# Interleaved activation tiles and weight units stored back to front in a two-layer encoder trunk

## The chip, the cores and the metric

The kernel runs on one core of a Trainium2 chip. A core has a matrix engine (TensorE, PE in the profile, with its weight loads shown as PEld), VectorE (DVE), ScalarE (ACT), GpSimd (POOL) and SyncE (SP), which issues most of the DMAs. The metric is the device time of one execution in microseconds, the median over several runs.

## The reference

The input is one sequence of 256 rows with 2048 channels, in float32. Two layers follow each other:

```python
u = rms_norm(h, g);  q, k, v, f = split(u @ a_w_in)            # layer A
o = forgetting_attention(q, k, v, cumsum(log_sigmoid(f + b)))  # 16 heads of 128
h = h + o @ a_w_out
h = h + square(relu(rms_norm(h, g) @ w1)) @ w2                 # 2048 -> 8192 -> 2048
k_sh, v_sh = split(rms_norm(h, g) @ kv_w)                      # shared by layer B
q = rms_norm(rms_norm(h, g) @ b_w_q)                           # layer B
h = h + chunked_relbias_attention(q, k_sh, v_sh, b_rel) @ b_w_out
h = h + square(relu(rms_norm(h, g) @ w1)) @ w2
```

Nearly all the work is in the projections with 2048 x 2048 blocks of weights. All of it is float32, and the result must be close to a float32 reference, which decides how the products are formed.

## The kernel before

**Splitting.** A float32 number is split in two parts: hi, the number rounded to the matrix engine's faster 32-bit format (float32r), and lo, the rest. A product of activations x and weights w is then three passes: x_hi with w_hi, x_lo with w_hi, x_hi with w_lo. The function `passes` (L485 to L495) issues them: L491, L493 and L495 in this order. The stationary operand, put into the array by a weight load before each matmul, is a 128 x 128 slice of the activations; the moving operand is a 128 x 512 slice of the weights; the result is a 128 x 512 accumulator.

**Activation tiles.** Activations lie transposed in tiles `[P, 2, GH, T]`: 128 partitions, two parts (hi, then lo), four row groups of 128 channels, 256 sequence positions. Four tiles hold the 16 row groups of one activation, and 60 tiles are made in all. They are filled at five places: `split_x` (L279, input, at the very start, one row group at a time just before its first use), `split_turned` (L312, the activations after each normalisation), `values` (L662, attention output), `take` (L870, the hidden activations of an MLP) and `gates` (L739, not an activation but the small gate weights). ScalarE writes hi, VectorE computes lo as the difference, reading hi again. A weight load reads 128 neighbouring positions of one part and one row group. In `gates` the tiles are the moving operand (L758).

**Weight units.** Weights arrive by DMA in units of 128 x 1024 (`raw`, `UN` = 1024), two slices of 512. `issue` (L213) takes the next unit, lets ScalarE copy it rounded into `hi` (L227) and VectorE subtract into `lo` (L228), in three rotating buffers each, and puts the pair into the queue `ready`. `top_up` and `fetch` keep two to three split units ahead of the matmuls. `products` (L499) applies a plain unit to two blocks of 128 rows: two slices, two blocks, three passes, twelve matmuls.

**Formed units.** In the MLPs and the query projection, blocks of weights are combined in pairs by a seven-product scheme (class `Pair`, `form_products`, L518). For a part of the rows the weights are first added to each other (L848, or a DMA that adds), and such a sum is a formed unit (`Form`), split by the same two lines of `issue` under the names `w`, `wT` and `query`. Its stationary operands are the activation tiles in three of the seven products and sums of activations (`S`, `Sh`) in the other four. The pairs are 1536 wide (14 in all, formed over the first six row groups, the rest plain), 2048 wide (16, over the first eight) or 1024 wide (4, over the first four).

**Order.** The order of all units is written out by `plan_mlp`. Work beside the matmuls (norms, softmax, transposes) is put in small steps into the list `fill`, and one step is run after each unit. At the end `keep_order` fixes the written order of VectorE, ScalarE, TensorE and SyncE; the waits between engines come from the framework, which sees which instruction writes and reads which tile.

Of the kernel before, what the change touches and what calls it, by code (L numbers as in the profile page):

```python
# [10 lines left out]
F32R = mybir.dt.float32r  # L11
# [4 lines left out]
P = 128  # L16
T = 256
# [4 lines left out]
GH = 4  # L22
# [5 lines left out]
UN = 1024  # L28
# [22 lines left out]
def trunk(ctx: ExitStack, tc: tile.TileContext, xT, xr, gs, hg, bf, wgate, w_in, w_oa, w1a, w1fa, w1sa, w2fa, w2sa,  # L51
          w_kv, w_qb, w_ob, w1b, w1fb, w1sb, w2fb, w2sb, rel, out):
    nc = tc.nc
    V, S, G, TE, SY = nc.vector, nc.scalar, nc.gpsimd, nc.tensor, nc.sync

    def pool(name, bufs, **kw):
        return ctx.enter_context(tc.tile_pool(name=name, bufs=bufs, **kw))
# [3 lines left out]
    acts = pool("acts", 8)  # L61
# [33 lines left out]
    first = sm.tile([P, GH], F32, name="first", bufs=1)  # L95
# [100 lines left out]
    tail_b = Tail(w_ob, n_out - 5)  # L196
    plan_b = plan_mlp(w1b, w1fb, w1sb, w2fb, w2sb, tail_b)
    ready = deque()

    raws = deque()  # L200

# [11 lines left out]
    def issue(parts=1):  # L213
        form = None
        if not raws:
            load(parts)
        raw, cuts = raws.popleft()
        if not cuts:
            form, half = raw, raw.half
            raw, cuts = form.pair.t[form.name], [slice(0, form.pair.cols - UN if half else UN)]  # L220
            if half:
                raw = raw[:, UN:]
        n = cuts[-1].stop
        hi = wsp.tile([P, n], F32R, name="hi" if n == UN else "hih", bufs=3 if n == UN else 1)
        lo = wsp.tile([P, n], F32R, name="lo" if n == UN else "loh", bufs=3 if n == UN else 1)
        for c in cuts:
            S.activation(hi[:, c], raw[:, c], AF.Copy)  # L227
            V.tensor_tensor(lo[:, c], raw[:, c], hi[:, c].bitcast(F32), op=ALU.subtract)  # L228
        ready.append((hi, lo, n < UN))
        if form and form.pair.deep and form.name == "T3":  # L230
            make(form.pair, "T2", int(half))
        elif form and half == form.pair.wide:
            if form.name == "T3":
                make(form.pair, "T2")
            elif form.name == "T2" and form.pair.adds:
                put(form.pair, "T4")
# [33 lines left out]
        return [ps_acc.tile([P, 512], F32, name="acc", tag=f"acc{which}{b}", bufs=1) for b in range(NB)]  # L270

    part = [None]

    def quarter(m):
        if m % GH == 0:
            part[0] = acts.tile([P, 2, GH, T], F32R, name="act")
        return part[0][:, :, m % GH, :]

    def split_x(src, m, which):  # L279
# [29 lines left out]
    def room(tag, name, dtype=F32):  # L309
        return qkv.tile([P, DEEP], dtype, name=name, tag=tag, bufs=1)  # L310

    def split_turned(t, n, which, into, fs=None):  # L312
        x = acts.tile([P, 2, GH, T], F32R, name="act")
        y = room("bias", "y").rearrange("p (a t) -> p a t", a=GH)[:, :, :T]
        for j in range(GH):
            m = which * KT + GH * n + j
            S.activation(y[:, j].rearrange("p (b i c) -> p b i c", b=NB, i=4), t[:, j], AF.Copy, scale=gsb[:, m : m + 1])
            if j == 1:
                yield
        S.activation(x[:, 0], y, AF.Copy)  # L320
        V.tensor_tensor(x[:, 1], y, x[:, 0].bitcast(F32), op=ALU.subtract)  # L321
        into.extend(x[:, :, j, :] for j in range(GH))
        yield
        if fs is not None:
            w = (GH - 2 * n) * T
            fs.extend(qkv.tile([P, w], F32R, name="S", tag="sS"[n], bufs=2) for _ in range(2))
            yield from sums([[y[:, j : GH - 2 * n : 2, b * P : (b + 1) * P] for j in range(2)] for b in range(NB)], fs[2 * n :], 2 - n)
# [157 lines left out]
    def passes(items, hi, lo, cols=slice(0, 512), **kw):  # L485

        def cut(w, j):
            return w[:, j * 512 + cols.start : j * 512 + cols.stop]

        for ps, (xh, _), j, first, _ in items:  # L490
            TE.matmul(ps[:, cols], xh, cut(hi, j), start=first, stop=False, **kw)  # L491
        for ps, (_, xl), j, _, _ in items:
            TE.matmul(ps[:, cols], xl, cut(hi, j), start=False, stop=False, **kw)  # L493
        for ps, (xh, _), j, _, last in items:
            TE.matmul(ps[:, cols], xh, cut(lo, j), start=False, stop=last, **kw)  # L495
# [206 lines left out]
    x = []  # L702
# [35 lines left out]

    def gates(x, st):  # L739
        r3 = wgr.rearrange("p (k c) -> p k c", k=KT)  # L740
        w = acts.tile([P, 2, GH, T], F32R, name="act")
        w3 = w.rearrange("p i a t -> p (i a t)").rearrange("p (k c) -> p k c", k=KT)
        box = []

        def clear():
            G.memset(w.bitcast(F32), 0.0)
            G.memset(early[:H, 3 * T : 4 * T], 1.0)

        def parts():
            h3, l3 = w3[:, :, :H], w3[:, :, 32 : 32 + H]  # L750
            S.activation(h3, r3, AF.Copy)
            V.tensor_tensor(l3, r3, h3.bitcast(F32), op=ALU.subtract)

        def products(ks):
            if not box:
                box.append(ps_s.tile([P, 512], F32, name="s"))
            for k in ks:
                TE.matmul(box[0], w3[:, k], x[k], start=k == 0, stop=k == KT - 1)  # L758

        c = early[:H, 2 * T : 3 * T]  # L760

        def logs():
            z = wk.tile([H, T], F32, name="gz", tag="wk")
            u = wk.tile([H, T], F32, name="gu", tag="wk")
            S.activation(z, box[0][:H, T:], AF.Copy)
            V.tensor_tensor(u, box[0][:H, :T], z, op=ALU.add)
            S.activation(z, box[0][32 : 32 + H, :T], AF.Copy)
            V.tensor_tensor(u, u, z, op=ALU.add)
            V.tensor_tensor(u, u, st.R[:H, :], op=ALU.mult)
            V.tensor_scalar(u, u, bfb, None, op0=ALU.add)  # L770
            V.scalar_tensor_tensor(z, u, -1.0, u, op0=ALU.mult, op1=ALU.max)
            yield
            S.activation(z, z, AF.Exp, scale=-1.0)
            S.activation(z, z, AF.Ln, bias=1.0)
            yield
            V.scalar_tensor_tensor(z, u, 0.0, z, op0=ALU.min, op1=ALU.subtract)
            V.tensor_tensor_scan(c, early[:H, 3 * T : 4 * T], z, 0.0, op0=ALU.mult, op1=ALU.add)
            yield
            nct = wk.tile([H, REL], F32, name="nct", tag="wk")
            V.tensor_scalar(nct[:, 0:P], c[:, 0:P], -1.0, None, op0=ALU.mult)  # L780
            V.tensor_scalar(nct[:, P:], c, -1.0, None, op0=ALU.mult)
            ct["cd"] = dram.tile([H, REL], F32, name="cd")
            G.dma_start(ct["cd"], nct)
            yield

        def turn_c():
            pc = ps_o.tile([P, 512], F32, name="pt", tag="po")
            ct["cq"] = const.tile([P, NB, H], F32, name="cq")
            for b in range(NB):
                TE.transpose(pc[:, b * H : (b + 1) * H], c[:, b * P : (b + 1) * P], ident[:H, :H])  # L790
            V.tensor_copy(ct["cq"].rearrange("p b h -> p (b h)"), pc[:, : NB * H])

        step, spread = steps(logs), steps(st.spread)
        return [[clear], [], [parts], [lambda: products(range(8))], [lambda: products(range(8, KT))], [spread], [spread],
                [step], [step], [step], [step], [turn_c]]
# [69 lines left out]
    def mlp(plan, x, Sx, st, last, more=None):  # L865
# [3 lines left out]

        def take(t, c, n):  # L870
            S.activation(t, t, AF.Relu)
            y = acts.tile([P, 2, GH, T], F32R, name="act")
            hi, lo = (y[:, i].rearrange("p k (b i c) -> p (k b) i c", b=NB, i=4) for i in range(2))
            t3 = t.rearrange("p (i kb c) -> p kb i c", i=4, c=32)
            yield
            S.activation(hi, t3, AF.Square)
            yield
            S.activation(t, t, AF.Square)
            yield

            def low():
                V.tensor_tensor(lo, t3, hi.bitcast(F32), op=ALU.subtract)

            hids[c].extend(y[:, :, j, :] for j in range(GH))
            low()
            yield
            if n == 0:
                r = prob.tile([P, 4 * UN], F32R, name="Sh", tag="p", bufs=1)
                Sh[c].extend(r[:, i : i + n] for i, n in ((0, UN), (UN, UN), (2 * UN, UN), (3 * UN, UN)))
                yield from sums([[t3[:, 2 * j + b :: 4] for j in range(2)] for b in range(NB)], Sh[c])  # L890
            elif n == 1:
                yield from sums([[t3[:, 2 * j + b :: 4] for j in range(2)] for b in range(NB)], Sh[c][2:])
# [34 lines left out]
        for i, (p, q, u) in enumerate(plan):  # L927
            hi, lo = ready.popleft()[:2] if q > 1 and ready and not p.deep else fetch()
# [185 lines left out]
```

## Time and profile before

| what | value |
|---|---|
| median of 2 runs | 2098.87 us (2098.66 to 2099.08) |
| profiled execution, first to last instruction | 2090.4 us |
| median above the profiled execution's span | 8.5 us |
| TensorE matmuls | 9182, busy 2076.3 us |
| weight loads | 9182, busy 1709.6 us |
| VectorE busy | 1679.5 us |
| ScalarE busy | 1288.4 us |
| mean DMA rate | 261 GB/s |

The page of the profile gives for each engine its busy time and its share of the span. Matmuls are pipelined, so the lengths of neighbours overlap; the distance between two starts is the better measure of TensorE's pace. A group of instructions is told with its line, engine, operation, what it writes and reads by the program's names, its shape, its count, its busy time, the mean length of one in ns, and after the bar the time for which the engine sat idle just before, with what ended it.

### The profile page before, as it was taken

The numbers are of one execution on the slowest core, as the hardware profiler recorded it, in microseconds if no ns is written. First come the engines' busy times: TensorE is split into PE (matmuls) and PEld (weight loads), VectorE is DVE, ScalarE is ACT, GpSimd is POOL, SyncE is SP. The second block draws the span as 40 slices with busy tenths as digits, with TensorE's granted clock in tenths as the row PEclk, the third lists the DMA queues.
The fourth block names the chain that finished last, engine by engine and source line by source line (L and its number), as shares of the span: only waits on it lengthen the run. The fifth ranks groups of instructions, "written<-read, shape, count | busy, mean of one in ns | idle before, by whom it ended". The sixth has DMA issues, their size and how long they took to land.

```text
span 2090.4 us, 26489 instructions
## 1 busy us (share of the span) xinstructions
PE 2076.3 (99%) x9182; PEld 1709.6 (82%) x9182; DVE 1679.5 (80%) x1972; ACT 1288.4 (62%) x1613; POOL 150.1 (7%) x195
## 2 busy tenths in 40 slices
PE   9999999999999999999999999999999999999999
PEld 7888888878887887887878888888788788878877
DVE  5767666889789889889988577778988897898886
ACT  6544454767567667667776445556765675676674
POOL 1111000001001001001011001000010010010010
PEclk9999999999999999999999999999999999999999
DMA  7777778789689789788878777787987986897885
GB/s 285 248 253 240 232 255 264 250 268 296 232 292 283 241 270 298 231 273 287 280 252 269 233 232 234 247 264 266 294 280 233 284 284 232 291 286 237 274 279 182
DMA packets 176151, 545.14 MB, mean 261 GB/s; under 512 B 37760, under 2 KB 70416, under 8 KB 163728
## 3 DMA queue, kind: packets, MB, share of 16 engines
q1 hardware_dynamic: 163088, 477.31, 64.4%
q0 software_dynamic: 12640, 65.57, 16.2%
q8 instruction: 72, 1.18, 0.2%
q14 instruction: 63, 0.52, 0.1%
q10 hardware_dynamic: 288, 0.57, 0.1%
HBM read 503.49 MB, written 35.68 MB: 258 GB/s over the span
## 4 chain that ended last, share of the span: by engine, by line
PE 86%; DVE 5%; DMA 5%; ACT 2%; issue 2%; SPq 1%; ACTq 0%; DVEq 0%
PE acc L491 22%; PE acc L493 22%; PE acc L495 22%; PE s L495 6%; PE s L491 5%; PE s L493 5%; DVE lo L228 3%; DMA turn<-z 2%; DMA raw<-in_w1sa 1%; ACT hi L227 1%; PE s L635 1%; PE po L665 1%; DVE z L341 1%; DMA raw<-in_w1sb 1%; SPq L357 0%
## 5 line engine op out<-in xcount | busy, mean ns | idle before, releaser
L228 DVE TENSOR_TENSOR lo<-raw,hi 128x1024 fp32r<-128x1024 f32 (+1 forms) x542 | 655.2, 1214 | 189.3 <-ACT hi L227 176.1
L227 ACT ACTIVATE hi<-raw 128x1024 fp32r<-128x1024 f32 (+1 forms) x542 | 569.3, 1053 | 311.3 <-PE acc L493 232.4
L491 PE MATMUL acc<-hi,act 128*128 128x512 f32 x2092 | 580.4, 394 | 1.3 <-ACT hi L227 1.3
L495 PE MATMUL acc<-lo,act 128*128 128x512 f32 x2092 | 571.6, 390 | 0.0
L493 PE MATMUL acc<-hi,act 128*128 128x512 f32 x2092 | 571.0, 389 | 0.1
L493 PEld LDWEIGHTS acc<-hi,act 128*128 128x128 f32 x2092 | 392.7, 188 | 83.0 <-DVE act L321 0.7
L495 PEld LDWEIGHTS acc<-lo,act 128*128 128x128 f32 x2092 | 391.3, 188 | 84.6 <-DVE lo L228 3.4
L491 PEld LDWEIGHTS acc<-hi,act 128*128 128x128 f32 x2092 | 390.5, 188 | 82.0 <-ACT hi L227 3.2
L227 ACT ACTIVATE hi<-w 128x1024 fp32r<-128x1024 f32 x202 | 212.7, 1057 | 93.4 <-PE acc L493 42.9
L228 DVE TENSOR_TENSOR lo<-w,hi 128x1024 fp32r<-128x1024 f32 x202 | 245.5, 1219 | 22.4 <-ACT hi L227 19.1
L228 DVE TENSOR_TENSOR lo<-wT,hi 128x1024 fp32r<-128x1024 f32 x142 | 172.2, 1221 | 60.8 <-ACT hi L227 59.1
L227 ACT ACTIVATE hi<-wT 128x1024 fp32r<-128x1024 f32 x142 | 148.1, 1055 | 74.4 <-PE acc L493 32.2
L495 PE MATMUL s<-lo,act 128*128 128x512 f32 x370 | 102.1, 392 | 6.0 <-DVE lo L228 6.0
L491 PE MATMUL s<-hi,act 128*128 128x512 f32 x370 | 101.1, 390 | 0.0
L493 PE MATMUL s<-hi,act 128*128 128x512 f32 x370 | 100.9, 389 | 0.0
L495 PEld LDWEIGHTS s<-lo,act 128*128 128x128 f32 x370 | 68.7, 188 | 23.8 <-DVE lo L228 10.1
L493 PEld LDWEIGHTS s<-hi,act 128*128 128x128 f32 x370 | 69.5, 188 | 14.4
L491 PEld LDWEIGHTS s<-hi,act 128*128 128x128 f32 x370 | 69.3, 188 | 14.5 <-ACT hi L227 0.3
L848 DVE TENSOR_TENSOR wT<-wT,w 128x1024 f32<-128x1024 f32 (+1 forms) x48 | 66.3, 1381 | 1.6
L668 ACT ACTIVATE act<-po 128x256 fp32r<-128x256 f32 x32 | 12.3, 385 | 88.0 <-PE po L666 88.0
L848 DVE TENSOR_TENSOR wT<-w,w 128x1024 f32<-128x1024 f32 (+1 forms) x48 | 65.5, 1364 | 0.3 <-DMA w<-in_w2fa 0.3
L577 POOL TENSOR_TENSOR ss<-ss,mhalf 128x4 f32<-128x4 f32 x32 | 43.5, 1367 | 271.8 <-DVE ss L576 271.8
(209 smaller groups left out, 1968.8 us busy)
## 6 DMA issues: line engine op xcount, KB each, us to landing
raw<-in_w_in SPq DMA_DIRECT2D x95, 512.0 KB, 4.6
raw<-in_w1sa SPq DMA_DIRECT2D x70, 512.0 KB, 6.4
raw<-in_w1sb SPq DMA_DIRECT2D x70, 512.0 KB, 6.1
w<-in_w2fa SPq DMA_DIRECT2D x32, 1024.0 KB, 7.7
raw<-in_w2sa SPq DMA_DIRECT2D x64, 512.0 KB, 8.0
raw<-in_w_kv SPq DMA_DIRECT2D x64, 512.0 KB, 4.7
w<-in_w2fb SPq DMA_DIRECT2D x32, 1024.0 KB, 7.5
raw<-in_w2sb SPq DMA_DIRECT2D x64, 512.0 KB, 7.3
```

The costliest lines, as they stand in the source:

```text
L227: S.activation(hi[:, c], raw[:, c], AF.Copy)
L228: V.tensor_tensor(lo[:, c], raw[:, c], hi[:, c].bitcast(F32), op=ALU.subtract)
L341: V.transpose(z.rearrange("p (j n b c) -> p b n j c", j=4, n=n, b=nb)[:, b], src.rearrange("p (n j c) -> p n j c", n=n, j=4))
L491: TE.matmul(ps[:, cols], xh, cut(hi, j), start=first, stop=False, **kw)
L493: TE.matmul(ps[:, cols], xl, cut(hi, j), start=False, stop=False, **kw)
L495: TE.matmul(ps[:, cols], xh, cut(lo, j), start=False, stop=last, **kw)
L577: G.tensor_tensor(rn, vv, mhalf, op=ALU.pow)
L635: TE.matmul(s[:, P : 3 * P], q[:, a, P:T], k[:, a], start=True, stop=True)
L665: TE.matmul(po[:, :T], v[:, 0, a * P : (a + 1) * P], pT[:, :2], start=True, stop=False)
L668: S.activation(o[i][:, 0], po[:, :T], AF.Copy)
L848: V.tensor_tensor(d, a, b, op=ALU.add)
```

## The change

Two layouts are altered. First, a helper `new_act` makes the activation tiles, and every second one is laid out as `[P, GH, T, 2]`: the hi and the lo part of one element lie next to each other. The code sees it through a view with the old order of axes, so one part is read and written with a step of two elements. The tile in `gates` keeps its layout and stays in the same rotation. Second, plain weight units of the whole width are counted, and where the count leaves 0 or 1 after division by four, `hi` and `lo` are replaced by views that run backwards. ScalarE and VectorE then store the unit back to front, and the matmuls read it back to front, so that the elements come in the same order as before. These matmuls are issued by a copy of the three loops in `passes`, on lines of their own. The number of instructions, the order of the work, the buffers and the DMAs in the code are the same.

```diff
@@ -196,6 +196,7 @@
     tail_b = Tail(w_ob, n_out - 5)
     plan_b = plan_mlp(w1b, w1fb, w1sb, w2fb, w2sb, tail_b)
     ready = deque()
+    count, back = [0], {}
 
     raws = deque()
 
@@ -223,6 +224,11 @@
         n = cuts[-1].stop
         hi = wsp.tile([P, n], F32R, name="hi" if n == UN else "hih", bufs=3 if n == UN else 1)
         lo = wsp.tile([P, n], F32R, name="lo" if n == UN else "loh", bufs=3 if n == UN else 1)
+        if n == UN and not form:
+            count[0] += 1
+            if count[0] % 4 < 2:
+                hi, lo = hi[:, ::-1], lo[:, ::-1]
+                back[id(hi)] = hi
         for c in cuts:
             S.activation(hi[:, c], raw[:, c], AF.Copy)
             V.tensor_tensor(lo[:, c], raw[:, c], hi[:, c].bitcast(F32), op=ALU.subtract)
@@ -270,10 +276,18 @@
         return [ps_acc.tile([P, 512], F32, name="acc", tag=f"acc{which}{b}", bufs=1) for b in range(NB)]
 
     part = [None]
+    kinds = [0]
+
+    def new_act():
+        i = kinds[0] % 2
+        kinds[0] += 1
+        if i:
+            return acts.tile([P, GH, T, 2], F32R, name="alt", tag="act").rearrange("p a t i -> p i a t")
+        return acts.tile([P, 2, GH, T], F32R, name="act", tag="act")
 
     def quarter(m):
         if m % GH == 0:
-            part[0] = acts.tile([P, 2, GH, T], F32R, name="act")
+            part[0] = new_act()
         return part[0][:, :, m % GH, :]
 
     def split_x(src, m, which):
@@ -310,7 +324,7 @@
         return qkv.tile([P, DEEP], dtype, name=name, tag=tag, bufs=1)
 
     def split_turned(t, n, which, into, fs=None):
-        x = acts.tile([P, 2, GH, T], F32R, name="act")
+        x = new_act()
         y = room("bias", "y").rearrange("p (a t) -> p a t", a=GH)[:, :, :T]
         for j in range(GH):
             m = which * KT + GH * n + j
@@ -487,6 +501,14 @@
         def cut(w, j):
             return w[:, j * 512 + cols.start : j * 512 + cols.stop]
 
+        if id(hi) in back:
+            for ps, (xh, _), j, first, _ in items:
+                TE.matmul(ps[:, cols], xh, cut(hi, j), start=first, stop=False, **kw)
+            for ps, (_, xl), j, _, _ in items:
+                TE.matmul(ps[:, cols], xl, cut(hi, j), start=False, stop=False, **kw)
+            for ps, (xh, _), j, _, last in items:
+                TE.matmul(ps[:, cols], xh, cut(lo, j), start=False, stop=last, **kw)
+            return
         for ps, (xh, _), j, first, _ in items:
             TE.matmul(ps[:, cols], xh, cut(hi, j), start=first, stop=False, **kw)
         for ps, (_, xl), j, _, _ in items:
@@ -738,7 +760,7 @@
 
     def gates(x, st):
         r3 = wgr.rearrange("p (k c) -> p k c", k=KT)
-        w = acts.tile([P, 2, GH, T], F32R, name="act")
+        w = acts.tile([P, 2, GH, T], F32R, name="act", tag="act")
         w3 = w.rearrange("p i a t -> p (i a t)").rearrange("p (k c) -> p k c", k=KT)
         box = []
 
@@ -869,7 +891,7 @@
 
         def take(t, c, n):
             S.activation(t, t, AF.Relu)
-            y = acts.tile([P, 2, GH, T], F32R, name="act")
+            y = new_act()
             hi, lo = (y[:, i].rearrange("p k (b i c) -> p (k b) i c", b=NB, i=4) for i in range(2))
             t3 = t.rearrange("p (i kb c) -> p kb i c", i=4, c=32)
             yield
```

## The prediction

> **What bounds the kernel now.** First the page's busy times and the granted clock, then the chain that ended last, then what TensorE waited for.
>
> ```profile
> span 2090.4 us, 26489 instructions
> PE 2076.3 (99%) x9182; PEld 1709.6 (82%) x9182; DVE 1679.5 (80%) x1972; ACT 1288.4 (62%) x1613; POOL 150.1 (7%) x195
> ...
> PEclk9999999999999999999999999999999999999999
> ...
> PE 86%; DVE 5%; DMA 5%; ACT 2%; issue 2%; SPq 1%; ACTq 0%; DVEq 0%
> ```
>
> ```profile
> PE s L495 <- DVE lo L228: 7.0, 10, 0.9
> PE acc L491 <- ACT hi L227: 1.3, 1, 1.3
> PE pt L92 <- DVE mhalf L94: 1.1, 1, 1.1
> ```
>
> TensorE is busy 99% of the span at the full clock, and its listed waits are 7.0 + 1.3 + 1.1 = 9.4 us. So the time is a count of matmuls times the distance from one start to the next. That distance is read in the timeline of a steady stretch (columns: start, length of the group, engine, line, operation, count). Matmul lengths overlap, so I take starts.
>
> ```profile
> 302.23 1.07 PE L495 MATMUL acc<-lo,act 128*128 128x512 f32 x4
> 303.13 1.07 PE L491 MATMUL acc<-hi,act 128*128 128x512 f32 x4
> 304.04 1.07 PE L493 MATMUL acc<-hi,act 128*128 128x512 f32 x4
> 304.95 1.07 PE L495 MATMUL acc<-lo,act 128*128 128x512 f32 x4
> ```
>
> From 302.23 to 304.95 there are twelve starts: 2.72 / 12 = 0.2267 us, 227 ns per matmul. Times 9182 that is 2081 us, the whole span. The share that grows with the number of columns comes from two shapes of one line:
>
> ```profile
> L493 PE MATMUL acc<-hi,act 128*128 128x512 f32 x2088 | 570.1, 390 | 0.1
> L493 PE MATMUL acc<-hi,act 128*128 128x256 f32 x4 | 0.8, 283 | 0.0
> ```
>
> 256 more columns take 107 ns, so 512 take 214 ns, and about 13 ns of the 227 do not depend on the columns. Weight loads run beside this stream:
>
> ```profile
> 300.18 0.87 PEld L491 LDWEIGHTS acc<-hi,act 128*128 128x128 f32 x4
> 301.10 0.87 PEld L493 LDWEIGHTS acc<-hi,act 128*128 128x128 f32 x4
> ```
>
> ```profile
> 299.74 0.38 PE L634 MATMUL s<-k,q 128*128 128x128 f32 x2
> 299.85 0.30 PEld L635 LDWEIGHTS s<-k,q 128*128 128x128 f32 x2
> ```
>
> ```profile
> L634 PE MATMUL s<-k,q 128*128 128x128 f32 x64 | 12.2, 272 | 0.0
> ...
> L635 PEld LDWEIGHTS s<-k,q 128*128 128x128 f32 x64 | 9.7, 192 | 0.0
> ```
>
> Among long matmuls four loads of 188 ns fill 0.87 us, one per 227 ns, at the matmuls' pace. Among the short ones of the attention, two loads fill 0.30 us, so their starts lie 0.30 - 0.19 = 0.11 us apart, and so do the matmuls' (0.38 - 0.27). A load thus needs at most 110 ns of its own; beside a 512-column matmul it has 227 - 110 = 117 ns to spare.
>
> **The change part by part.** It adds no instruction, DMA or queue entry and moves none; SP's and POOL's queues carry the same items in the same order. It alters the addresses of operands.
>
> How many are touched follows from the loops and these rows:
>
> ```profile
> L228 DVE TENSOR_TENSOR lo<-raw,hi 128x1024 fp32r<-128x1024 f32 x538 | 652.6, 1218 | 188.3 <-ACT hi L227 175.1 <-PE acc L493 9.3 <-PE s L493 0.7
> ...
> L228 DVE TENSOR_TENSOR lo<-raw,hi 128x512 fp32r<-128x512 f32 x4 | 2.6, 686 | 1.0 <-ACT hi L227 1.0
> ```
>
> 538 whole units and two written in halves are 540 plain units; two of every four are 270. Each feeds twelve matmuls (three passes, two slices, two row blocks): **3240 matmuls** read their moving operand backwards. Activation tiles come in fours, and the second and fourth are interleaved. Plain units meet these in 112 of 224 units outside the planned pairs, 84 of 140 in the 1536-wide pairs (row groups 6 to 15 of 16), 64 of 128 in the 2048-wide ones (8 to 15) and 32 of 48 in the narrow ones (4 to 15): 292 units, 3504 weight loads. The second halves of the formed units add 14 x 9 + 16 x 18 = 414. So **3918 weight loads** step by 8 bytes.
>
> *Step of 8 bytes in a weight load.* No row here has such a load. Below: nothing, as now. It may double to 220 ns and still fit into 227. At four times, 440 ns, the pace would be its own: 213 ns x 3918 = +835 us. A gain is limited to the 13 fixed ns, 3918 x 13 = -51 us. I take 0: nearest is the load of at most 110 ns, which would have to more than double before anything shows. If that cover were gone, each further 10 ns would cost 39 us.
>
> [...]
>
> *Moving operand backwards.* No matmul of the trace reads so; two other engines do. VectorE copies the identity reversed (L477), beside a plain copy source of the same size (L467), and ScalarE reads the query room forwards for one normalisation and backwards for the other, eight times each (L317; shortest, median, longest):
>
> ```profile
> L477 DVE COPY flipper<-ident x1: 221/221/221, 1074.8 to 1074.8; 128x128 f32<-128x128 f32 x1
> ```
>
> ```profile
> L467 DVE COPY rb<-rx x2: 218/220/221, 48.0 to 48.1; 128x128 f32<-128x128 f32 x2
> ```
>
> ```profile
> L317 ACT ACTIVATE y<-query,gsb x16: 491/494/497, 1066.4 to 1124.4; 128x256 f32<-128x256 f32 x16
> ```
>
> 221 beside 220 ns, and 491 to 497 over both directions: a backward read is free there. Those engines take one element per ns or so, TensorE one per 107 / 256 = 0.42 ns, so the rows do not prove it for TensorE. Bounds: 0, and half the rate, 214 ns x 3240 = +693 us; a gain is again limited to the fixed part, 3240 x 13 = -42 us. I take 0, by these rows. Eight of the sixteen gate matmuls (L758) get an interleaved moving operand; at half rate that is 8 x 214 ns = 1.7 us.
>
> *Writes.* 270 times ScalarE writes hi and VectorE writes lo backwards, and 30 of the 60 activation tiles are written, and hi read again, with the step of 8 bytes.
>
> ```profile
> L227 ACT ACTIVATE hi<-raw 128x1024 fp32r<-128x1024 f32 x538 | 567.0, 1056 | 310.4 <-PE acc L493 232.4 <-PE s L493 31.6 <-DMA raw<-in_w_in 13.5
> ```
>
> ```profile
> L882 DVE TENSOR_TENSOR act<-q,act 128x1024 fp32r<-128x1024 f32 x32 | 39.1, 1223 | 12.6 <-ACT q L878 11.8 <-DMA w<-in_w2fb 0.8
> ```
>
> L882 reads its source in blocks of 32 and takes 1223 ns, as long as L228 with straight operands (1218): the time goes by element, not by address. I take 0 here too. At half the rate the 270 lo would add 270 x 1.2 = 324 us to VectorE. Outside the MLP that is covered; inside it is not:
>
> ```profile
> core 0: us, PE busy (x) PEld busy (x) DVE busy (x) ACT busy (x) POOL busy (x), PEclk, DMA share, GB/s
> ...
> 440.00:640.00 200.00, 197.60 (x863) 160.77 (x862) 172.08 (x180) 130.11 (x147) 11.71 (x17) 1.00 0.84 271
> 640.00:840.00 200.00, 199.32 (x875) 163.30 (x875) 172.53 (x174) 131.81 (x145) 16.66 (x26) 1.00 0.86 275
> ```
>
> VectorE has some 27 us idle in each 200. An MLP has 12 + 70 + 64 = 146 plain units in about 650 us, 73 of them reversed, 22 per 200 us: 22 x 1.2 = 27 us more would use up all of it.
>
> *Waits.* Interleaved halves of one tile cover the same address range. If the ordering treats that range as one, TensorE's first pass, which needs only hi, also waits for VectorE's lo. Later stages have their tiles long before use; only at the start does a tile come just in time, and only two of its four tiles are interleaved: four steps by the length of L284, 0.48 us, are 1.9 us at most:
>
> ```profile
> L284 DVE SCALAR_TENSOR_TENSOR act<-xin,gsb,act 128x256 fp32r<-128x256 f32 x16 | 7.0, 480 | 4.5 <-ACT act L283 4.5
> ```
>
> Queued behind such a wait on TensorE are only the later matmuls, which are the path itself. I take 1 us of it.
>
> **The sum.** 2090.4 + 0 + 0 + 0 + 1 = 2091.4 us of span. The median of 2098.87 is 8.5 us over the profiled span, so **2100 us**: no change that could be measured. About 2% (42 us) is what a measurement of this kernel can tell from none.
>
> **The rivals.**
>
> *Loads disturb the stream (ends slower).* The 13 fixed ns may be the weight load's reads taking turns with the moving operand's. If twice the span of addresses takes twice the turns, every strided load adds 13 ns: 3918 x 13 = 51 us, **2151 us**, +2.4%. It decides as soon as the extra passes 42 us / 3918 = 11 ns. For it: the fixed part is the same in every clean group. Against it: no row has a different load beside a long matmul. [...]
>
> *The backward stream is slower.* From one more fixed part per matmul (3240 x 13 = +42 us, 2142) to half rate (+693 us, **2793**), with anything between: a quarter of the rate lost, 71 ns each, gives 2330. For it: TensorE takes elements more than twice as fast as the engines whose backward reads are shown. Against it: those rows show no cost at all.
>
> *Backward writes slow VectorE.* At half rate the MLP has no VectorE time left; if half of 2 x 73 x 1.22 = 178 us comes through, 89 us, **2190 us**. Against it: L882 beside L228.
>
> *Strided loads take over twice their time.* At four times, +835 us, about **2935 us**. Against it: the spare 117 ns.
>
> *Faster.* Only the fixed part and the waits can go: 51 us or 42 us, at best about **2050 us**. Nothing in the profile speaks for it.
>
> *The change does not do what it says*, if the reversed view were undone in storing: then nothing changes, and the time is the forecast's.
>
> **How the numbers follow.** No change 0.38 (own range 2090 to 2112); loads disturb the stream 0.18; slower backward stream 0.22, of which 0.12 below 2400; slower writes 0.10; loads over twice 0.06; faster 0.06, half of that within 2%. The single likeliest case is no change, so 2100 is the time, though the slower cases together hold more. A range from 2085 to 2400 holds 0.38 + 0.18 + 0.12 + 0.10 + 0.03 = 0.81. Over 2% slower: 0.18 + 0.22 + 0.06 and 0.08 of the writes are 0.54; over 2% faster 0.03; within 2% the rest, 0.43.
>
> **What would show it.** The reversed matmuls have lines of their own (L506, L508, L510, 1080 each), the others L513, L515, L517. Right: starts 227 ns apart on both sets of lines, L227 and its VectorE partner still near 1056 and 1218 ns, waits of TensorE near 9 us. Loads that disturb: some 240 ns between starts on half of both sets. A slower stream: only L506 to L510 stretch. Slower writes: TensorE's wait for lo grows tenfold and VectorE passes 90% in the MLP. The forecast is wrong if TensorE's reads cost by address rather than by element; that is the step with the least evidence.

## The result and the profile after

The changed kernel takes 2127.65 us (2127.34 to 2127.96), before 2098.87 us: a ratio of 1.0144, 95% interval 1.0115 to 1.0174. That is slower, clear of noise, and less than 2%. The profiled execution lasted 2125.6 us from first to last instruction and 2127.34 us in all.

First the page of the changed kernel, with the busy times and the granted clock, then what its TensorE waited for (us in total, times, longest).

```profile
span 2125.6 us, 26489 instructions
PE 2114.3 (99%) x9182; PEld 1737.8 (82%) x9182; DVE 1680.2 (79%) x1972; ACT 1290.9 (61%) x1613; POOL 151.5 (7%) x195
...
PEclk9999999999999999999999999999999999999999
...
L234 DVE TENSOR_TENSOR lo<-raw,hi 128x1024 fp32r<-128x1024 f32 (+1 forms) x542 | 655.4, 1214 | 202.2 <-ACT hi L233 196.8
L233 ACT ACTIVATE hi<-raw 128x1024 fp32r<-128x1024 f32 (+1 forms) x542 | 569.0, 1052 | 325.8 <-PE acc L515 134.0
```

```profile
PE s L517 <- DVE lo L234: 4.4, 8, 0.9
PE acc L506 <- ACT hi L233: 1.2, 1, 1.2
PE pt L92 <- DVE mhalf L94: 1.1, 1, 1.1
```

The instructions are the same in number, the granted clock is the same (1.000 in both), TensorE is still busy 99% of the span, and it waits less (6.7 us) than before (9.4 us). VectorE and ScalarE split a plain unit in 1214 and 1052 ns, before in 1214 and 1053, although half of these are now written backwards. So TensorE waits for nothing longer: the matmuls themselves follow each other more slowly. The timeline of the changed kernel shows it. L506 to L510 read backwards, L513 to L517 forwards; `act` is an old activation tile, `alt` an interleaved one.

```profile
262.43 1.10 PE L508 MATMUL acc<-hi,act 128*128 128x512 f32 x4
263.36 1.10 PE L510 MATMUL acc<-lo,act 128*128 128x512 f32 x4
264.29 1.09 PE L513 MATMUL acc<-hi,act 128*128 128x512 f32 x4
265.22 1.07 PE L515 MATMUL acc<-hi,act 128*128 128x512 f32 x4
266.12 1.07 PE L517 MATMUL acc<-lo,act 128*128 128x512 f32 x4
267.03 0.59 PE L687 MATMUL po<-pbuf,v 128*128 128x256 f32 x2
...
268.62 1.09 PE L515 MATMUL acc<-hi,alt 128*128 128x512 f32 x4
269.55 1.09 PE L517 MATMUL acc<-lo,alt 128*128 128x512 f32 x4
270.49 1.10 PE L506 MATMUL acc<-hi,alt 128*128 128x512 f32 x4
271.42 1.10 PE L508 MATMUL acc<-hi,alt 128*128 128x512 f32 x4
272.36 0.86 PE L510 MATMUL acc<-lo,alt 128*128 128x512 f32 x3
```

Forwards from old tiles, 265.22 to 267.03, eight matmuls take 1.81 us, 226 ns each. Backwards from old tiles, 262.43 to 264.29, eight take 1.86 us, 233 ns each. With interleaved tiles it is 233 to 234 ns in both directions (268.62 to 272.36, sixteen in 3.74 us). Over the trace from 13 us on, for matmuls of 512 columns that are followed by one of the same kind, distance from start to start:

```
changed kernel            pairs   median ns   mean ns (without gaps over 260 ns)
forwards,  old tile        1887   227         227.9
forwards,  interleaved     1957   233         233.3
backwards, old tile        1368   233         233.4
backwards, interleaved     1606   233         233.5
forwards,  sums (S, Sh)    1232   227         228.5
```

In the trace of before, old tiles and sums both have 227 ns. An interleaved tile costs 6.7 ns, a backward unit costs 6.7 ns, and a matmul that has both pays once. By the counts of the trace 1500 matmuls read backwards with an old tile, beside the 3918 strided loads: 5418 x 6.67 = 36 us. The two profiled spans differ by 2125.6 - 2090.4 = 35.2 us. The medians differ by less, 28.8 us; the profiled execution before was among its faster ones, as more runs of that kernel show below.

Two small things stand beside it, both in the changed kernel: ScalarE's writes with the step of 8 bytes, and the gate matmuls, whose moving operand is an activation tile (for these the three numbers are shortest, median and longest in ns).

```profile
L898 ACT ACTIVATE alt<-q 128x1024 fp32r<-128x1024 f32 x16 | 18.6, 1162 | 0.0
L898 ACT ACTIVATE act<-q 128x1024 fp32r<-128x1024 f32 x16 | 16.8, 1047 | 0.1
```

```profile
L904 DVE TENSOR_TENSOR alt<-q,alt 128x1024 fp32r<-128x1024 f32 x16 | 19.6, 1227 | 14.1 <-ACT q L900 14.1
L904 DVE TENSOR_TENSOR act<-q,act 128x1024 fp32r<-128x1024 f32 x16 | 19.5, 1219 | 0.0
```

```profile
L780 PE MATMUL s<-act x8: 387/392/399, 40.8 to 47.1; 128*128 128x512 f32 x8
...
L780 PE MATMUL s<-alt,act x8: 615/629/630, 41.7 to 48.6; 128*128 128x512 f32 x8
```

An interleaved tile takes ScalarE 115 ns longer to write and VectorE 8 ns; the list of TensorE's waits above shows none for it. In the timeline the gate matmuls whose moving operand has a step of 8 bytes start 448 ns apart (four in 1.79 us, from 41.75 us on), before 227: some 220 ns longer, on eight matmuls, 1.8 us in all.

### The profile page after: what moved, and what is told of

Read it like the earlier page. It is cut to its first block, busy times and chain, and to the rows that moved or that the text cites. A ratio compares the mean times of both kernels' runs of the same rounds, so it can differ in the third digit from the quotient of the medians.

```text
span 2125.6 us, 26489 instructions
## 1 busy us (share of the span) xinstructions
PE 2114.3 (99%) x9182; PEld 1737.8 (82%) x9182; DVE 1680.2 (79%) x1972; ACT 1290.9 (61%) x1613; POOL 151.5 (7%) x195
## 4 chain that ended last, share of the span: by engine, by line
PE 86%; DMA 5%; DVE 4%; ACT 2%; issue 1%; SPq 0%; ACTq 0%; DVEq 0%
PE acc L515 14%; PE acc L513 14%; PE acc L517 14%; PE acc L506 9%; PE acc L510 9%; PE acc L508 9%; PE s L517 4%; PE s L513 4%; PE s L515 4%; DVE lo L234 2%; PE s L506 2%; PE s L510 2%; PE s L508 2%; DMA turn<-z 1%; DMA raw<-in_w1sa 1%
## 5 line engine op out<-in xcount | busy, mean ns | idle before, releaser
L234 DVE TENSOR_TENSOR lo<-raw,hi 128x1024 fp32r<-128x1024 f32 (+1 forms) x542 | 655.4, 1214 | 202.2 <-ACT hi L233 196.8
L233 ACT ACTIVATE hi<-raw 128x1024 fp32r<-128x1024 f32 (+1 forms) x542 | 569.0, 1052 | 325.8 <-PE acc L515 134.0
L513 PE MATMUL acc<-hi,act 128*128 128x512 f32 x598 | 170.6, 395 | 0.0
L517 PE MATMUL acc<-lo,act 128*128 128x512 f32 x598 | 167.4, 390 | 0.0
L515 PE MATMUL acc<-hi,act 128*128 128x512 f32 x598 | 167.3, 390 | 0.1
L513 PE MATMUL acc<-hi,alt 128*128 128x512 f32 x576 | 162.9, 398 | 0.0
L517 PE MATMUL acc<-lo,alt 128*128 128x512 f32 x576 | 161.2, 395 | 0.0
L515 PE MATMUL acc<-hi,alt 128*128 128x512 f32 x576 | 161.0, 394 | 0.0
L506 PE MATMUL acc<-hi,alt 128*128 128x512 f32 (+1 forms) x490 | 136.6, 401 | 0.0
L510 PE MATMUL acc<-lo,alt 128*128 128x512 f32 (+1 forms) x490 | 135.0, 397 | 0.0
L508 PE MATMUL acc<-hi,alt 128*128 128x512 f32 (+1 forms) x490 | 134.4, 396 | 0.0
L513 PEld LDWEIGHTS acc<-hi,act 128*128 128x128 f32 x598 | 111.6, 188 | 25.3 <-ACT hi L233 0.5
L515 PEld LDWEIGHTS acc<-hi,act 128*128 128x128 f32 x598 | 112.2, 188 | 24.6 <-DVE act L335 0.5
L517 PEld LDWEIGHTS acc<-lo,act 128*128 128x128 f32 x598 | 111.9, 188 | 24.0 <-DVE lo L234 0.5
L517 PEld LDWEIGHTS acc<-lo,alt 128*128 128x128 f32 x576 | 111.0, 193 | 23.6 <-DVE lo L234 0.7
L515 PEld LDWEIGHTS acc<-hi,alt 128*128 128x128 f32 x576 | 111.2, 193 | 23.2 <-DVE alt L335 0.2
L513 PEld LDWEIGHTS acc<-hi,alt 128*128 128x128 f32 x576 | 111.1, 194 | 21.6 <-ACT hi L233 0.3
L506 PE MATMUL acc<-hi,act 128*128 128x512 f32 x428 | 120.0, 403 | 1.2 <-ACT hi L233 1.2
```

## The experiments

**The two halves, and the whole again.** Theory A: each matmul with a strided load or a backward operand pays 6.67 ns, once. Rival B: the two costs are separate and add up. Rival C: the backward units carry all of it. Interleaving alone:

```diff
-            if count[0] % 4 < 2:
+            if False:
```

> Interleaved tiles alone; all weight units forwards. Theory A (in the changed kernel's trace a matmul starts 233.3 ns after the last, not 226.7, when its weight load steps by 8 bytes or its moving operand runs backwards, and 233.3 also when both hold): 3918 loads x 6.67 ns = +26 us over before. Theory B (the two costs are separate and add up to the whole of +29 us, in proportion to 3918 and 3240): +16 us. Theory C (the backward units carry it, by their matmuls or their writers): 0.

Backward units alone:

```diff
-        if i:
+        if False:
             return acts.tile([P, GH, T, 2], F32R, name="alt", tag="act").rearrange("p a t i -> p i a t")
```

> Backward units alone; all activation tiles in the old layout. Theory A: 3240 matmuls x 6.67 ns = +22 us. Theory B: +13 us. Theory C: +29 us. Under A the two runs together come to 48 us, about 12 us (1746 matmuls that are both) more than the whole change; under B they come to the whole change.

The changed kernel without an edit, on the same chip:

> The changed kernel again, beside the two halves on one chip. Theory A: 3918 + 1500 = 5418 matmuls x 6.67 ns = +36 us, less what stalls elsewhere give back. Theories B and C: +29 us.

Against 2095.63 us before (eleven runs from 2090.77 to 2100.73), interleaving alone took 2115.93 us, ratio 1.0096 (1.0079 to 1.0113), +20 us; backward units alone 2114.69 us, ratio 1.0087 (1.0071 to 1.0102), +19 us; both 2127.13 us, ratio 1.0150 (1.0130 to 1.0170), +31.5 us. Each is 3 to 6 us under theory A. Rival C falls: interleaving alone costs. The halves come to 39 us, 8 us more than the whole. That is the side of theory A (12 us more) and not of B (nothing more), but the intervals, some 4 us to either side, do not settle it. In the trace of interleaving alone the interleaved loads have 233.3 ns from start to start and the rest 227; in that of backward units alone it is the backward matmuls that have 233.5.

**All units backwards, without and with interleaved tiles.** This sets the two readings far apart: if the costs add, interleaving on top of 540 backward units costs another 26 us; if a matmul pays once, 3 us.

```diff
-            if count[0] % 4 < 2:
+            if True:
```

The first of the two runs has the old layout of the tiles besides.

> All 540 plain weight units backwards, all activation tiles in the old layout: 6480 matmuls. Theory A (6.67 ns per touched matmul): 6480 x 6.67 = +43 us over before. A cost that came from alternating between the two directions would not grow: +20 us as with half of the units.

> All plain units backwards and every second tile interleaved. Theory A (a matmul that has both pays once): only the 414 strided loads of the formed units come on top of all units backwards, 414 x 6.67 = 3 us: +46 us. Rival (the two costs add): 3918 x 6.67 = 26 us on top: +69 us.

Against 2094.89 us before: all backwards 2131.3 us, ratio 1.0169 (1.0155 to 1.0183), +36 us; all backwards and interleaved 2135.06 us, ratio 1.0190 (1.0176 to 1.0204), +40 us. Interleaving adds 4 us, not 26: a matmul pays once. The doubled dose of backward units costs 36 us where half cost 19, so it is no matter of changing direction. Both stand 6 to 7 us under the 43 and 46 of theory A. In the traces, starts more than 260 ns apart exceed 230 ns by 24 us in all before, and by 17 and 18 us in these two. So some 5 to 7 us of stalls went, about what is missing. Slower matmuls leaving the other engines more time is a likely reason; it was not tried by itself.

**The matmul by itself.** Only matmuls on resident data, 24 of a kind on a line of its own, one weight load before each:

```python
for i in range(R): TE.matmul(ps, st(1, i), mv(1, 512), start=True, stop=True)    # L46
for i in range(R): TE.matmul(ps, st(2, i), mv(1, 512), start=True, stop=True)    # L47
...                                                                              # L48 to L50: stationary steps 4, 8, 3
for i in range(R): TE.matmul(ps, st(1, i), mv(-1, 512), start=True, stop=True)   # L51
...                                                                              # L52 to L54: the same with stationary steps 2, 4, 8
for i in range(R): TE.matmul(ps, st(1, i), mv(2, 512), start=True, stop=True)    # L55
```

`R` is 24; `st(k, i)` is a stationary operand and `mv(k, n)` a moving operand with a step of k elements, both float32r.

> Only matmuls on resident data, 24 of each kind on its own line: stationary operand with steps of 1, 2, 3, 4 and 8 elements, moving operand with steps of 1, -1, 2 and -2, 512, 384 and 256 columns, weight loads of 128, 64 and 32 columns, starts shifted by one or two elements. It leaves the whole computation of the reference out. Theory A: 227 ns for (1, 1), 233 for (2, 1), (1, -1) and (2, -1). If the fixed 13 ns are the weight load's reads taking turns with the moving operand, they halve with 64 columns and quarter with 32 (220 and 217 ns) and grow with the step (4: over 240 ns). If they are a start-up part that only grows with an awkward operand, they stay at 227 with 64 and 32 columns. If the extra belongs to columns, 256 columns backwards cost 3 ns; if it belongs to the matmul, 7 ns.

The timeline of that kernel; the pace of a line is the next line's start less its own, divided by 24.

```profile
25.40 5.61 PE L46 MATMUL ps<-mov,wgt 128*128 128x512 f32 x24
30.84 5.76 PE L47 MATMUL ps<-mov,wgt 128*128 128x512 f32 x24
36.44 5.81 PE L48 MATMUL ps<-mov,wgt 128*128 128x512 f32 x24
...
53.61 5.77 PE L51 MATMUL ps<-mov,wgt 128*128 128x512 f32 x24
59.21 5.76 PE L52 MATMUL ps<-mov,wgt 128*128 128x512 f32 x24
64.81 5.76 PE L53 MATMUL ps<-mov,wgt 128*128 128x512 f32 x24
...
76.36 11.00 PE L55 MATMUL ps<-mov,wgt 128*128 128x512 f32 x24
87.17 11.11 PE L56 MATMUL ps<-mov,wgt 128*128 128x512 f32 x24
...
126.17 3.04 PE L62 MATMUL ps<-mov,wgt 128*128 128x256 f32 x24
129.05 3.04 PE L63 MATMUL ps<-mov,wgt 128*128 128x256 f32 x24
131.92 5.77 PE L64 MATMUL ps<-mov,wgt 128*128 128x256 f32 x24
137.53 5.96 PE L65 MATMUL ps<-mov,wgt 128*128 128x256 f32 x24
143.32 3.01 PE L66 MATMUL ps<-mov,wgt 128*128 128x256 f32 x24
146.17 3.06 PE L67 MATMUL ps<-mov,wgt 128*128 128x256 f32 x24
...
149.06 5.69 PE L68 MATMUL ps<-mov,wgt 128*64 128x512 f32 x24
154.59 5.72 PE L69 MATMUL ps<-mov,wgt 128*64 128x512 f32 x24
```

Straight operands (L46): 5.44 / 24 = 227 ns. Stationary step 2 (L47): 5.60 / 24 = 233 ns. Backwards (L51) 233 ns, and backwards with stationary step 2 (L52) 233 ns as well. So the kernel's three numbers appear with no other engine at work, and the single payment too. A moving operand with step 2 (L55) takes 10.81 / 24 = 450 ns. With 256 columns (L62 to L65, stationary steps 1, 2, 4, 8) the pace is 120, 120, 234 and 241 ns: a load with step 2 fits under 120 ns, one with step 4 does not and by that pace needs about 234 ns of its own. So the prediction's cover was there for step 2, and would just have been gone at step 4. A load of half as many columns (L68) does not shorten the fixed part: 230 ns, more than the 227 with 128. Backwards with 256 columns (L66) is 119 ns, so nothing is paid there, where the expectation had 3 or 7 ns. Straight operands whose start is shifted by one or two elements (L73 to L75) gave 230 to 237 ns.

Two more kernels of the same kind varied length, start and type.

> Only matmuls again, the rest of the computation left out: 512 to 320 columns with straight operands, backwards moving operand, and interleaved stationary operand; starts shifted by 4 to 32 elements; the same in bfloat16. If the extra is paid per column, it shrinks in proportion with the columns (4.2 ns at 320); if a weight load and the moving operand get in each other's way, it comes and goes with the length and the start, without a simple proportion; if the number of bytes decides, bfloat16 shows no extra at a step of 2 and none backwards.

In the first, L69 to L76 read backwards with 512, 504, 496, 480, 448, 416, 384 and 320 columns, L61 to L68 forwards. L93 to L97 are bfloat16 with stationary steps 1, 2, 4 and then backwards with steps 1, 2; L98 and L99 have moving steps 2 and 4.

```profile
25.73 5.60 PE L61 MATMUL ps<-mov,wgt 128*128 128x512 f32 x24
31.17 5.60 PE L62 MATMUL ps<-mov,wgt 128*128 128x504 f32 x24
...
60.72 3.67 PE L68 MATMUL ps<-mov,wgt 128*128 128x320 f32 x24
64.23 5.77 PE L69 MATMUL ps<-mov,wgt 128*128 128x512 f32 x24
69.84 5.68 PE L70 MATMUL ps<-mov,wgt 128*128 128x504 f32 x24
...
99.86 3.69 PE L76 MATMUL ps<-mov,wgt 128*128 128x320 f32 x24
103.38 5.76 PE L77 MATMUL ps<-mov,wgt 128*128 128x512 f32 x24
...
186.76 5.35 PE L93 MATMUL ps<-movb,wgtb 128*128 128x512 bf16 x24
191.95 5.34 PE L94 MATMUL ps<-movb,wgtb 128*128 128x512 bf16 x24
197.13 5.34 PE L95 MATMUL ps<-movb,wgtb 128*128 128x512 bf16 x24
...
207.49 5.34 PE L97 MATMUL ps<-movb,wgtb 128*128 128x512 bf16 x24
212.67 5.58 PE L98 MATMUL ps<-movb,wgtb 128*128 128x512 bf16 x24
218.09 11.00 PE L99 MATMUL ps<-movb,wgtb 128*128 128x512 bf16 x24
```

At 512 columns backwards costs 6.7 ns over forwards (5.61 against 5.44 us for 24); at 320 it costs nothing (3.52 against 3.51 us). It is not paid per column in proportion. In bfloat16 neither a stationary step of 2 or 4 elements (L94, L95) nor reading backwards (L96; L97 has stationary step 2 besides) costs anything: 216 ns throughout. A moving step of 4 bytes (L98) gives 226 ns. A step of 8 bytes (L99) gives 451 ns between the starts within the line, about half the rate, as in float32r. (From L99 to the next line the trace has 10.41 us, 434 ns each, only because the first start of that line is recorded 46 ns after the last of L99.)

> Only matmuls on resident data, 512 float32r columns, the rest of the computation left out; the starts of the stationary and the moving operand are shifted by 32 to 1536 elements, and the backward and the interleaved operand are tried from other starts. If the 6.67 ns belong to the direction and the step as such, every backward and every interleaved line shows 233 ns and every straight one 227. If they come from how the two operand streams of TensorE fall on each other, straight operands at some starts cost as much (the run before had 229 to 233 ns at starts shifted by 4 to 32 elements), and backward operands at some start may cost nothing. With the weight load always from the same address nothing changes under either.

In the second, L51 to L54 shift the stationary operand by 32, 64, 96 and 128 elements, L55 to L66 the moving one by 48 to 1536, and L67 to L71 a backward one by 64 to 1024.

```profile
36.40 5.75 PE L51 MATMUL ps<-mov,wgt 128*128 128x512 f32 x24
41.99 5.62 PE L52 MATMUL ps<-mov,wgt 128*128 128x512 f32 x24
47.44 5.75 PE L53 MATMUL ps<-mov,wgt 128*128 128x512 f32 x24
53.03 5.62 PE L54 MATMUL ps<-mov,wgt 128*128 128x512 f32 x24
...
124.11 5.77 PE L67 MATMUL ps<-mov,wgt 128*128 128x512 f32 x24
129.72 5.76 PE L68 MATMUL ps<-mov,wgt 128*128 128x512 f32 x24
```

Straight weight loads shifted by 32 or 96 elements also cost 233 ns (5.59 / 24, L51 and L53); shifted by 64 or 128 they cost 227 ns (5.45 / 24, L52). Every moving start tried that is a multiple of 64 elements gave 227 ns, 48 and 96 gave 233; in the first of the two kernels, starts of either operand shifted by 1 to 32 elements gave 229 to 233. Backward operands gave 233 ns at every start tried here. So 227 ns is not the pace of a float32r matmul of which some patterns fall short by a price of their own: at 512 columns and with loads of 128 it is the pace when both operands run forwards without a step from a multiple of 64 elements (256 bytes) past the start of their tile, and everything else timed in these three kernels with loads of up to 8 bytes' step and a stream without gaps lies between 229 and 237 ns. (L100, backwards from a start shifted by one element, is left aside: its first start is the one recorded 46 ns after the last of L99.) That fits with two departures at once costing no more than one (backwards, step 2 and both together each 233 ns above). Which part of TensorE's read path does this is open. That a shifted or strided weight load slows a stream whose own reads are unchanged (233 beside 227 ns) shows that their paces are not independent. No version came out of this that is faster than before, since the long matmuls of before already have the favourable pattern.

## Why the prediction was right and wrong

**The bound** was read rightly: the time is 9182 times the distance between two starts, TensorE waits under 10 us, and a change matters as far as it alters that distance.

**The counts** were right: 1080 backward matmuls on each of three lines (1082 instructions, since the last group is issued in halves) and 3918 strided loads (3924 instructions for the same reason).

**Backward moving operand: "I take 0"** is the step that failed. It was taken from VectorE (221 beside 220 ns) and ScalarE (491 to 497 ns), and TensorE's rate being twice theirs was given only as a reservation. Of these rows L467 was misread besides: it copies one column broadcast over 128 (`to_broadcast`), so its 220 ns are no price of a plain forward read. The runs showed 6.67 ns per matmul at 512 columns, 19 us for 3240 of them.

**Strided weight load: "I take 0"** failed in the same way, with 20 us for 3918. The bound of 110 ns was read from the attention's loads, whose tiles are plain float32 and not float32r. Still the cover was real, some 107 ns (a pace of 120 ns at 256 columns with step 2), but it covers only the load's own length, not what the load does to the stream beside it. No run shows the 0: matmuls after strided loads start 233 ns apart, after straight ones 227. The rival "loads disturb the stream" had this the right way round and at twice the price, 13 ns, since it took the whole fixed part for turns of the load; loads of 64 columns, which leave 230 ns, show that the fixed part is not that. In float32r a step of 8 bytes costs a load's neighbour 6.7 ns and a moving operand half its rate (450 ns): the load's pattern alone changes the pace from 227 to 233 ns, while in bfloat16 it stays at 216 for load steps of 1, 2 and 4.

**Adding the costs up** as separate terms would have failed too: all backwards plus interleaving cost 4 us more than all backwards, not 26. The two rivals on TensorE's reads were each priced as if it came alone; both came, at a smaller price, and shared it.

**Writes at 0** were right for the backward ones (1214 and 1052 ns) and for VectorE; ScalarE pays 115 ns for an interleaved tile, hidden. **The wait of 1 us** at the start does not show: waits fell from 9.4 to 6.7 us.

**The 8.5 us around the span** were misread. Later executions lie 1.7 to 1.8 us over their spans (2127.34 against 2125.6), so the profiled one before took about 2092 us, while executions of before spread from 2090.8 to 2100.7. The rest of the 8.5 us was that spread, and a sum made on the span belongs beside the execution that was profiled.

Together: 2100 us with an own range to 2112 was too low by 28 us, because both prices of TensorE's reads were carried over from places that do not show them; the wider range of 2085 to 2400 and the band of 2% held. The band held by the size of the price and not by the argument: at the rival's 13 ns the 5418 matmuls would have added 70 us, over 3%. The prediction had named the place itself, TensorE's reads, as the step with the least evidence, and its sign of being right, starts 227 ns apart on both sets of lines, did not come.

## What to carry to other kernels

Where TensorE's pace is the bound, look at the operands' addresses: in float32r keep both the stationary and the moving operand straight, forwards and starting at a multiple of 64 elements of their tiles (here 227 ns at 512 columns, otherwise 229 to 237), and keep steps out of the moving operand (here 450 ns at a step of 8 bytes). A cost that hides behind a busy stream must be asked twice: whether it fits in time, and whether it slows the stream that hides it. Prices of an access pattern did not carry over here from one engine to another (ScalarE took 491 to 497 ns over both directions, TensorE 6.7 ns more for each backward matmul of 512 columns), and prices on one resource did not add (4 us more for both, not 26).

## What was not expected of the hardware

A float32r matmul of 512 columns with a load of 128 had a favourable pace of 226.7 ns and lay at 229 to 237 ns for the other starts and directions timed above and for loads of step 2; shifting a straight load by 32 elements cost some 6 ns (233 beside 227). Departures did not add: backwards with a load of step 2 took 233 ns, as each alone. In bfloat16 the pace was 216 ns in both directions of the stream and at load steps of 1, 2 and 4. A moving operand with a step of 8 bytes ran at about half rate in both types (450 and 451 ns). Loads of 64 columns instead of 128 made the pace longer, 230 ns beside 227, not shorter.
